# The 16 token-mixing gates of a decoder layer as pairs by a seven-product block scheme

## The chip, the cores and the metric

The kernel runs on one core of one Trainium2 chip. The metric is the device time of one execution in microseconds. The engines that the text names: PE (TensorE, matrix products, with weight loads shown apart as PEld), DVE (VectorE), ACT (ScalarE), POOL (GpSimd), and SP (SyncE), which issues most of the transfers. Each engine works off its own instructions in a fixed order.

## The reference, cut to what matters

One decoder layer for a prompt of 512 tokens with 16 meta tokens and for 8 short samples. The normalised input x (1024 channels) goes through one input projection `w_in`, from which differential attention and a gated delta rule with four heads are computed. Each of the two branches is projected back to 1024 channels, and both are merged by two gates per channel, which come from the same projection:

```python
z = x @ w_in                          # one projection, split into nine parts
...
gate_a, gate_b = sigmoid(z[C_GA:]), sigmoid(z[C_GB:])   # 1024 channels each
mix = gate_a * (attention @ w_branch_a) + gate_b * (delta_rule @ w_branch_b)
```

An output projection, and then a gated feed-forward layer with a short convolution, follow. The kernel takes the sigmoid by a tanh of half the argument. All is float32. So the gates are one matrix product: 2048 output channels by 1024 input channels by 578 tokens.

## The kernel before, in words

Tokens are columns, channels are partitions. There are 578 columns, kept in two halves: columns 0 to 256, and 256 to 578 (322 of them). A float32 value is held as the sum of two numbers of the shorter matmul format, hi and lo. `split` makes them: ACT casts the value to hi, and DVE subtracts hi from it to give lo (`whi` and `wlo` for weights, `xhi` and `xlo` for the input x). A product of 128 input channels with 128 output channels is then three matmuls: hi by hi, hi by lo and lo by hi. For 1024 input channels that makes 24 matmuls for each half of the tokens.

`gate(i)` computes 128 of the 2048 gate channels. It fetches the weights with two transfers of 256 KB (`wraw`), splits them, multiplies both halves into two accumulator banks of the kind "d" (`ps_d`; two exist in this stage), and ACT takes the tanh into a tile `gt`. There are 16 such columns, two for each of 8 output blocks m.

The order of the program is set in two steps. Two streams are merged while the program is written (`merge`): `main` with the attention prompt and then the four heads of the delta rule, and `rest` with the attention of the samples, the 16 gates, and `branch_a`, the branch projection of the attention. `merge` takes the next step from the stream that is furthest behind by estimated work, and passes over a stream that announced a delay. After that a list scheduler places each engine's instructions. The gates are mostly the work that fills PE while a head's chain of small dependent steps waits for other engines.

A head is two streams of its own: `gdn_project(h)` makes its queries, keys and values, and `gdn_chain(h)` does the rest. In the chain come Gram products of keys (`ps_g`), masks by decay on DVE (`dbig_low`, `dbig_up`, `lm`), a triangular substitution on DVE (the loop of L970 to L972 on `row` and `xc`, 15 rounds, each needing the one before), products with its result `xy` on PE, a recurrence over chunks (`gv`, `gS`, `grhs`, `st`), normalisation of the output `on`, transposes of it, and multiplication by the head's own gate z, which `gdn_gate` computes from x with 48 matmuls. The product `ob` is then split (`bhi`, `blo`). For each head, `gdn_gate` is called near the chain's end, ahead of the transposes of `on` in program order.

The input x as hi and lo lies in `self.x` and stays there until the gates are done. While head h's chain runs, `gdn_project(h + 1)` uses the buffers `pre`, `cy`, `q`, `kt` and `vt`; during the last head's chain they are free. `branch_a` puts the splits of the attention result `oa` into `pre`, `cy`, `q` and `qb`.

The feed-forward stage (`ffn_in`) already multiplies in blocks of two by two with seven products in place of eight; the sums of weight blocks it needs (`sw`, L1805) are made on POOL and DVE, and split afterwards (`hw`, `lw`).

Of the kernel before, what the change touches and what calls it, by code (L numbers as in the profile page):

```python
# [9 lines left out]
F32 = mybir.dt.float32  # L10
F32R = mybir.dt.float32r
I32 = mybir.dt.int32
AF = mybir.ActivationFunctionType
ALU = mybir.AluOpType
# [11 lines left out]
H = 4  # L26
# [8 lines left out]
NQ = SEQ + NS + 2  # L35
# [4 lines left out]
HALF_Q = ((0, 256), (256, 578))  # L40
# [99 lines left out]
WRAW, WLO = 3, 4  # L140
LOADS_AHEAD = 5
NC = 290
PLAIN = 3
TAILS = 4
FINE = 8
MAIN_1 = 600.0
# [4 lines left out]
class Body:  # L151
# [39 lines left out]
    def run(self):  # L191
        nc, ctx = self.nc, self.ctx
        self.cpool = self.pool(ctx, "cpool")
        self.wpool = self.pool(ctx, "wpool")
        self.small = self.pool(ctx, "small")
        self.dram = self.pool(ctx, "dram", space=bass.MemoryType.DRAM)
        self.consts = self.t(self.cpool, [128, _CONSTANTS.shape[1]], "consts")
        self.ident = self.consts[:, 0:128]
        nc.scalar.dma_start(self.ident, self.a["constants"][:, 0:128])
        self.mhalf = self.t(self.cpool, [128, 32], "mhalf")  # L200
        nc.vector.memset(self.mhalf, -0.5)
        self.x2d = self.t(self.dram, [NQ, D], "x2d")

        self.psum = self.pool(ctx, "psum", space=PSUM)
        self.banks, self.turn = "d", 0
        with ExitStack() as sm:
            with ExitStack() as s1:
                self.opool = self.pool(s1, "opool")
                self.oa = self.t(self.opool, [128, H, NQ], "oa")
                self.ob = self.t(self.opool, [128, H, NQ], "ob")  # L210
                with ExitStack() as s2:
                    self.keep = self.pool(s2, "keep")
                    self.x = self.parts(self.pool(s2, "xpool"), "x", 8, HALF_T)
                    with ExitStack() as s:
                        first = self.embed(self.pool(s, "embed", 2, side="right"))
                    self.gproj = self.pool(s2, "gproj")
                    da = ExitStack()
                    dpool = self.pool(da, "da")
                    self.psum_m = self.pool(da, "psum_m", space=PSUM)
                    self.da_queries(dpool, first)  # L220
                    with ExitStack() as s:
                        tmp = self.pool(s, "gs", side="right")
                        self.gdn_scalars(tmp)
                        self.gdn_consts(tmp)
                    self.news = self.chain = self.spare = False

                    def main():
                        head = {}
                        yield from self.da_main(dpool, self.gdn_project(0, head))
                        da.close()  # L230
                        self.chain = True
                        self.psum_g = self.pool(ctx, "psum_g", space=PSUM)
                        with ExitStack() as s:
                            self.gpool = self.pool(s, "gpool")
                            yield from self.gdn(head)
                        yield from self.mix_parts(self.pool(s2, "mix"))

                    def rest():
                        with ExitStack() as s:
                            yield from self.sample_attention(self.pool(s, "sa", side="right"))  # L240
                        self.gates, self.gtpool = {}, self.pool(sm, "gates", side="right")
                        for i in range(16):
                            yield from self.gate(i)
                        while not self.spare:
                            yield None
                        yield from self.branch_a()

                    self.drain(self.merge((main(), lambda: MAIN_2 if self.chain else MAIN_1), (rest(), REST_W)))
                    self.banks = "ggsttdd"
                    swo = ExitStack()  # L250
                    wo0 = self.wout_tiles(self.pool(swo, "wo0", side="right"), 0)
                    self.mix(wo0)
            sf = ctx.enter_context(ExitStack())
            fx = self.pool(sf, "fx")
            self.f = {
                key: tuple(self.t(fx, [128, 4, NC], f"f{p}{key}", F32R) for p in ("hi", "lo")) for key in ("11", "12", "21", "22")
            }
            for key in ("12", "22"):
                for e in self.f[key]:
                    nc.scalar.copy(e[:, :, 32:34], self.c("zero").unsqueeze(2).to_broadcast([128, 4, 2]))  # L260
            with ExitStack() as s:
                firsts = self.out_proj(self.pool(s, "wout"), wo0, swo, sm)
            self.ffn_in(firsts, sf, self.pool(sm, "gx", side="right"))
            sf.close()
            with ExitStack() as s1:
                self.ffn_out(self.pool(s1, "gh"), self.pool(s1, "fo"), self.pool(s1, "w3"))
# [399 lines left out]
    def gdn(self, head):  # L666
        pool = self.gpool
        self.zk = self.t(pool, [128, NB * 136], "zk")
        self.nc.gpsimd.memset(self.zk, 0.0)
        heads = [head] + [{} for _ in range(H - 1)]  # L670
        for h in range(H):
            streams = [(self.gdn_chain(h, heads[h]), 29.4)]
            if h + 1 < H:
                streams.append((self.gdn_project(h + 1, heads[h + 1]), 18.0))
            yield from self.merge(*streams)

    def gdn_project(self, h, st):
# [22 lines left out]
    def gdn_gate(self, h, z2):  # L700
        nc = self.nc
        wt = self.weight(self.a["w_in"][0], C_Z + 128 * h)
        for half in HALF_Q:
            out = []
            yield from self.dense_steps(wt, self.x, half, out)
            for p, c in out:
                zh = z2[:, c[0] : c[1]]
                nc.scalar.activation(zh, p, AF.Tanh, scale=0.5)
                nc.vector.scalar_tensor_tensor(out=zh, in0=zh, scalar=1.0, in1=p, op0=ALU.add, op1=ALU.mult)
            yield 0.0  # L710

    def gdn_chain(self, h, st):
        nc, pool, a, o = self.nc, self.gpool, self.a, self.o
        q, kt, vt = st["q"], st["kt"], st["vt"]
        C4 = [128, 4, 128]

        def cols(ap, h=h):
# [7 lines left out]
            out=gu, in0=self.c("upper").unsqueeze(1).to_broadcast(C4), in1=cols(self.g), op=ALU.mult  # L725
# [9 lines left out]
        for big, sign in (("big_low", -1.0), ("big_up", 1.0)):  # L735
            m = self.t(pool, [NTL, NTL], "dt" + big)
            nc.vector.scalar_tensor_tensor(
                out=m, in0=rt[:NTL, :NTL], scalar=self.gc[:NTL, 4, h : h + 1], in1=self.c(big + "_t", NTL),
# [9 lines left out]
        for big, sign in (("big_low", -1.0), ("big_up", 1.0)):  # L748
            m = self.t(pool, C4, "d" + big)
# [3 lines left out]
        last = self.t(pool, [128, 12], "elast")  # L753
# [32 lines left out]
        for e in range(2):  # L786
# [7 lines left out]
            out=kn[:, 0:4], in0=kn[:, 0:4], in1=kc[:, 0:4].unsqueeze(2).to_broadcast(C4), op=ALU.mult  # L794
        )
        yield DELAY[4]
        p = self.ps("t")
# [3 lines left out]
        p = self.ps4("t")  # L801
# [24 lines left out]
        y, at = res["yt"], res["att"]  # L826
        p = self.ps("g")
        for b in range(NB):
# [5 lines left out]
            out=rhs[:64], in0=p[:64, :128], scalar=self.neg_eg[:64, 4, h : h + 1], in1=vn[:64, 4],  # L834
# [6 lines left out]
        p = self.ps("g")  # L841
        self.mm(p[:NTL, :128], y, rhs[:NTL], start=True, stop=True)
        v = self.t(pool, [128, 128], "gv", bufs=2)
        nc.scalar.copy(v[:NTL], p[:NTL, :128])
        yield DELAY[7]
        p = self.ps("g")
# [3 lines left out]
        p = self.ps("g")  # L850
# [7 lines left out]
        for half in range(2):  # L858
# [3 lines left out]
                out=vm[:64],  # L862
                in0=v[:64].unsqueeze(1).to_broadcast([64, 4, 128]),
                in1=self.c("blocks_s", 64)[:, b4].unsqueeze(2).to_broadcast([64, 4, 128]),
                op=ALU.mult,
# [11 lines left out]
        for i in range(4):  # L877
            sl = slice(128 * i, 128 * i + 128)
            p = self.ps("g")
# [3 lines left out]
                out=rhs, in0=p[:, :128], scalar=self.neg_eg[:, i, h : h + 1], in1=vn[:, i], op0=ALU.mult, op1=ALU.add  # L883
# [30 lines left out]
            out=on[:, 0:4], in0=on[:, 0:4], in1=f[:, 0:4].unsqueeze(2).to_broadcast(C4), op=ALU.mult  # L914
        )
        nc.vector.tensor_scalar(on[:NTL, 4], on[:NTL, 4], f[:NTL, 4:5], None, op0=ALU.mult)
        z2 = self.t(pool, [128, NQ], "z2")
        yield from self.gdn_gate(h, z2)
        p = self.ps4("t")
        for i in range(4):  # L920
            self.transpose(p[:, i], on[:, i])
# [563 lines left out]

    GATES = ((C_GB, "w_branch_b"), (C_GA, "w_branch_a"))

    def gate(self, i):
        m, j = divmod(i, 2)
        th = self.t(self.gtpool, [128, NQ], "gt", bufs=18)  # L1490
        wt = self.weight(self.a["w_in"][0], self.GATES[j][0] + 128 * m)
        for half in HALF_Q:
            out = []
            yield from self.dense_steps(wt, self.x, half, out, 4)
            for p, c in out:
                self.nc.scalar.activation(th[:, c[0] : c[1]], p, AF.Tanh, scale=0.5)
            yield 0.0
        self.gates[i] = th

    def branch(self, m, j, x, half):  # L1500

# [707 lines left out]
```

## Time and profile before

| | |
|---|---|
| time, median of three runs | 1155.24 us (1153.86 to 1158.56) |
| the profiled execution | 1153.75 us, its span 1152.0 us |
| granted clock, mean | 0.996 |
| PE busy | 1115.3 us of the span |
| gates (tanh of the first to that of the last) | 493.6 to 620.4 us |
| feed-forward, the stretches of it read below | 800 to 1000 us |

A row of a group names line, engine, operation, output and inputs by the program's names, shape and count; then follow the busy time in total and the mean duration in nanoseconds, and then idle time of the engine before these instructions with what ended it. A row of a timeline begins with the start time and the duration in microseconds; a bracket at its end gives the idle time before it. A row of the stretches gives, for a window of the span, its length and each engine's busy time, the granted TensorE clock, and the transfers' share and rate.

### The profile page before, as it was taken

The numbers are of one execution on the slowest core, as the hardware profiler recorded it, in microseconds if no ns is written. First come the engines' busy times: TensorE is split into PE (matmuls) and PEld (weight loads), VectorE is DVE, ScalarE is ACT, GpSimd is POOL, SyncE is SP. The second block draws the span as 40 slices with busy tenths as digits, with TensorE's granted clock in tenths as the row PEclk, the third lists the DMA queues.
The fourth block names the chain that finished last, engine by engine and source line by source line (L and its number), as shares of the span: only waits on it lengthen the run. The fifth ranks groups of instructions, "written<-read, shape, count | busy, mean of one in ns | idle before, by whom it ended". The sixth has DMA issues, their size and how long they took to land.

```text
span 1152.0 us, 23616 instructions
## 1 busy us (share of the span) xinstructions
PE 1115.3 (97%) x8683; PEld 1004.1 (87%) x8683; DVE 717.3 (62%) x1875; ACT 539.0 (47%) x1308; POOL 220.5 (19%) x342
## 2 busy tenths in 40 slices
PE   6999999999999999999999999999999999999997
PEld 5887887787787787789999977899999999999996
DVE  5456666695486377474343765499889889832323
ACT  5334445464464365352332344365565656732321
POOL 2022221020120010010000003333455444200000
PEclk9999999999999999999999999999999999999999
DMA  7366335737756956823232364323333332432322
GB/s 208 81 223 188 102 104 195 255 110 251 237 159 216 290 173 209 263 74 80 55 90 69 110 187 153 95 70 102 102 87 100 93 94 73 144 97 74 102 75 83
DMA packets 184347, 157.56 MB, mean 137 GB/s; under 512 B 12570, under 2 KB 146273, under 8 KB 184231
## 3 DMA queue, kind: packets, MB, share of 16 engines
q1 hardware_dynamic: 179713, 147.53, 42.0%
q0 software_dynamic: 3264, 5.16, 1.5%
q10 hardware_dynamic: 1254, 3.35, 1.0%
q8 instruction: 69, 1.13, 0.4%
q14 instruction: 47, 0.39, 0.1%
HBM read 146.12 MB, written 9.88 MB: 135 GB/s over the span
## 4 chain that ended last, share of the span: by engine, by line
PE 73%; issue 13%; DVE 6%; ACT 3%; POOL 3%; DMA 1%; SPq 0%; DVEq 0%; POOLq 0%; ACTq 0%
PE ps_d L272 26%; PE ps_t L272 18%; PE ps_g L272 15%; PE ps_s L272 7%; PE ps_t L420 7%; ACT KT L1399 1%; PE ps_m L272 1%; DVE cy L650 1%; DMA lk<-in_da_lambda_k 1%; POOL grr L384 1%; POOL gf L384 0%; DVE wlo L315 0%; DMA page<-in_cache_v 0%; POOL hss L384 0%; DVE row L970 0%
## 5 line engine op out<-in xcount | busy, mean ns | idle before, releaser
L272 PE MATMUL ps_d<-xhi,whi 128*128 128x256 f32 (+2 forms) x704 | 217.8, 310 | 0.2 <-DVE qm L1128 0.2
L315 DVE TENSOR_TENSOR wlo<-wraw,whi 128x512 fp32r<-128x512 f32 x196 | 137.9, 720 | 122.4 <-ACT whi L314 121.6
L272 PE MATMUL ps_d<-xhi,wlo 128*128 128x256 f32 (+2 forms) x704 | 213.3, 303 | 0.7 <-DVE wlo L315 0.7
L272 PE MATMUL ps_d<-xlo,whi 128*128 128x256 f32 (+2 forms) x704 | 212.8, 303 | 0.3 <-DVE xlo L315 0.2
L314 ACT CAST whi<-wraw 128x512 fp32r<-128x512 f32 (+1 forms) x198 | 117.3, 612 | 179.1 <-PE ps_d L272 93.8
L272 PEld LDWEIGHTS ps_d<-xhi,whi 128*128 128x128 f32 x704 | 133.6, 190 | 5.8 <-issue 4.2
L272 PEld LDWEIGHTS ps_d<-xlo,whi 128*128 128x128 f32 x704 | 133.9, 190 | 3.3 <-issue 2.4
L272 PEld LDWEIGHTS ps_d<-xhi,wlo 128*128 128x128 f32 x704 | 133.6, 190 | 2.5 <-issue 1.0
L1399 ACT COPY KT<-ps_t 128x512 f32<-128x512 f32 x106 | 57.2, 603 | 31.3 <-PE ps_t L420 30.8
L420 PE MATMUL ps_t<-consts,page 128*128 128x128 f32 x512 | 67.8, 279 | 0.3
L272 PE MATMUL ps_t<-fhit,hw 128*128 128x290 f32 x228 | 68.0, 298 | 0.0
L272 PE MATMUL ps_t<-flot,hw 128*128 128x290 f32 x228 | 67.7, 297 | 0.0
L272 PE MATMUL ps_t<-fhit,lw 128*128 128x290 f32 x228 | 67.6, 297 | 0.0
L420 PEld LDWEIGHTS ps_t<-consts,page 128*128 128x128 f32 x512 | 55.6, 140 | 13.8 <-issue 6.7
L314 ACT CAST hw<-sw 128x512 fp32r<-128x512 f32 x76 | 47.2, 622 | 41.4 <-PE ps_g L272 19.9
L315 DVE TENSOR_TENSOR lw<-sw,hw 128x512 fp32r<-128x512 f32 x76 | 60.1, 790 | 6.7 <-ACT hw L314 6.6
L272 PEld LDWEIGHTS ps_t<-flot,hw 128*128 128x128 f32 x228 | 43.2, 190 | 0.0
L272 PEld LDWEIGHTS ps_t<-fhit,lw 128*128 128x128 f32 x228 | 43.1, 189 | 0.0
L272 PEld LDWEIGHTS ps_t<-fhit,hw 128*128 128x128 f32 x228 | 43.0, 189 | 0.0
L1887 DVE SCALAR_TENSOR_TENSOR fy<-fpre,fw,fy 128x592 f32<-128x592 f32 x44 | 36.5, 830 | 2.5 <-ACT fy L1885 1.8
L272 PE MATMUL ps_s<-page,pT 128*32 128x256 f32 x512 | 35.3, 385 | 1.8 <-DMA page<-in_cache_v 1.6
L272 PE MATMUL ps_s<-KT,qb 128*32 128x256 f32 x512 | 35.7, 385 | 0.6
(688 smaller groups left out, 2990.1 us busy)
## 6 DMA issues: line engine op xcount, KB each, us to landing
page<-in_cache_k SPq DMA_DIRECT2D x128, 256.0 KB, 4.2
page<-in_cache_v SPq DMA_DIRECT2D x128, 256.0 KB, 4.4
wraw<-in_w_in SPq DMA_DIRECT2D x88, 256.0 KB, 3.0
wraw<-in_w_ffn_in SPq DMA_DIRECT2D x50, 256.0 KB, 3.0
wraw<-in_w_down SPq DMA_DIRECT2D x40, 256.0 KB, 3.2
raw<-in_w_ffn_in SPq DMA_DIRECT2D x38, 256.0 KB, 2.9
wraw<-in_w_out SPq DMA_DIRECT2D x16, 256.0 KB, 2.9
x<-in_x_prompt SPq DMA_DIRECT2D x4, 512.0 KB, 8.7
```

Of the source, the lines that this page charges most:

```text
L272: return self.nc.tensor.matmul(out, lhsT, rhs, **kw).ins
L314: self.nc.scalar.copy(hi, raw)
L315: (eng or self.nc.vector).tensor_tensor(out=lo, in0=raw, in1=hi.bitcast(F32), op=ALU.subtract)
L384: nc.gpsimd.tensor_tensor(out=dst, in0=dst, in1=self.mhalf[:rows, :n], op=ALU.pow)
L420: self.nc.tensor.transpose(out, in_, self.ident[:k, :k])
L650: nc.vector.scalar_tensor_tensor(out=y, in0=pre[:, j : j + n], scalar=self.cw[:, ch, 24 + j : 25 + j], in1=y, op0=ALU.mult, op1=ALU.add)
L1399: copy(kt[:, :, 128 * j : 128 * j + 128], tp)
L1887: nc.vector.scalar_tensor_tensor(out=y, in0=pre[:, j : j + 592], scalar=fw[:, m, 16 + j : 17 + j], in1=y, op0=ALU.mult, op1=ALU.add)
```

## The change

The gates are computed in pairs of columns (2n, 2n+1) by a block scheme of seven products. The weights of a pair are four blocks: lower and upper half of the input channels for each of the two columns. The tokens are two blocks, X1 (columns 256 to 578, of which the first 256 take part in the scheme) and X2 (columns 0 to 256), again with lower and upper channels.

In round 1, `begin(n)` multiplies the lower half of column 2n with X1 into a bank and ACT copies this to the tile of column 2n+1; `end(n)` adds the upper half onto the same bank, and ACT takes the tanh, which finishes columns 256 to 578 of column 2n. Meanwhile POOL computes sums and differences of the token blocks (`sums`, `more`), first in rooms borrowed from `pre`, `cy`, `q`, `qb` and two gate tiles; they are split into `t3`, the `vt` buffer, and x's own blocks, which they overwrite (the scheduler orders this behind the last use).

In round 2, POOL makes four sums of weight blocks for each pair (`loads`), each is split as before (`divided`), and five products follow: two into bank A with 322 columns, one with 256, and two into bank C (`ps_s`) with 256. After each of them DVE adds the bank, as far as it has come, to what stands in the tiles (L1645, L1648, L1651, L1654, L1658), and ACT takes the remaining tanhs. The weights of round 2 are fetched a second time, with four transfers of 256 KB for each pair.

Since x is overwritten, head 3's own gate has to be computed before: `last_gate` runs as a stream beside the beginning of head 3's chain, and `rest` waits for it (`self.free`) before any gate is begun. The unchanged matmul helper, L272 before, has line 275 after; `split` moves from L314 and L315 to L317 and L318.

```diff
@@ constants
+AHEAD = 1
@@ run
-                        for i in range(16):
-                            yield from self.gate(i)
+                        while not self.free:
+                            yield None
+                        with ExitStack() as s:
+                            yield from self.all_gates(self.pool(s, "t3", side="right"))
@@ gdn
                 streams.append((self.gdn_project(h + 1, heads[h + 1]), 18.0))
+            else:
+                streams.append((self.last_gate(heads[h]), 18.0))
@@
+    def last_gate(self, st):
+        st["z2"] = self.t(self.gpool, [128, NQ], "z2")
+        yield from self.gdn_gate(H - 1, st["z2"])
+        self.free = True
@@ gdn_chain
-        z2 = self.t(pool, [128, NQ], "z2")
-        yield from self.gdn_gate(h, z2)
+        z2 = st.get("z2")
+        if z2 is None:
+            z2 = self.t(pool, [128, NQ], "z2")
+            yield from self.gdn_gate(h, z2)
@@
-    def gate(self, i):
...
-            yield from self.dense_steps(wt, self.x, half, out, 4)
-            for p, c in out:
-                self.nc.scalar.activation(th[:, c[0] : c[1]], p, AF.Tanh, scale=0.5)
+    def all_gates(self, pool):
...
+        def product(ps, wt, x, n, first, last, k0=0):
...
+            for k in range(4):
+                self.mm(ps[:, :n], hi[k], xhi[k0 + k][:, 0:n], start=first and k == 0, stop=False, **kw)
+                self.mm(ps[:, :n], hi[k], xlo[k0 + k][:, 0:n], start=False, stop=False, **kw)
+                self.mm(ps[:, :n], lo[k], xhi[k0 + k][:, 0:n], start=False, stop=last and k == 3, **kw)
...
+        def sums(e):
...
+            op(r12, raw(h2, ks, c), raw(l2, ks, c), ALU.add)
+            op(r11, raw(h1, ks, c), raw(l1, ks, c), ALU.add)
+            op(r11, r12, r11)
+            yield
+            op(r22, raw(h2, us, c), raw(l2, us, c), ALU.add)
+            op(r12, r22, r12)
+            op(r22, r22, r11)
+            yield
+            self.split(t3[e], t3[2 + e], r12)
+            self.split(h2[:, ks, c], l2[:, ks, c], r11)
+            op(r21, raw(h1, us, c), raw(l1, us, c), ALU.add)
+            op(r21, r21, r22)
+            yield
+
+        def later(e, j):
...
+            self.split(h1[:, ks, c], l1[:, ks, c], r)
...
+        def begin(n):
+            wt = self.weight(w, column(2 * n))
+            ps = self.ps("d")
+            product(ps, (wt[0][:4], wt[1][:4]), X1, N1, True, True)
+            nc.scalar.copy(th[2 * n + 1][:, 256:NQ], ps[:, :N1])
+            p1s[n] = ps, wt
+
+        def end(n):
+            ps, wt = p1s.pop(n)
+            product(ps, (wt[0][4:], wt[1][4:]), X1, N1, False, True, 4)
+            nc.scalar.activation(th[2 * n][:, 256:NQ], ps[:, :N1], AF.Tanh, scale=0.5)
+
+        def loads(n):
...
+            op(s1, a21, a22, ALU.add)
+            op(a21, a11, a21)
+            op(a11, s1, a11)
+            op(a12, a12, a11)
+            return {"s1": s1, "s3": a21, "s2": a11, "s4": a12, "22": a22}
+
+        begin(0)
+        yield 0.0
+        for n in range(1, 8):
+            begin(n)
+            yield 0.0
+            next(work, None)
+            next(work, None)
+            if n == 5:
+                ready.append(loads(0))
+            if n == 7:
+                for e in range(2):
+                    later(e, 0)
+            end(n - 1)
+            yield 0.0
...
+        end(7)
+        yield 0.0
+        for e in range(2):
+            later(e, 1)
+        self.split(h1[:, upper, c], l1[:, upper, c], more)
...
+        for n in range(8):
+            A, C = self.ps("d"), self.ps("s")
...
+            product(A, next(wts), X1, N1, True, True)
+            v.tensor_tensor(out=b1, in0=A[:, :N2], in1=p1, op=ALU.add)
+            yield 0.0
+            product(C, next(wts), X2, N2, True, True)
+            v.tensor_tensor(out=b2, in0=C[:, :N2], in1=p1, op=ALU.add)
+            yield 0.0
+            product(A, next(wts), X3, N2, False, True)
+            v.tensor_tensor(out=b2, in0=A[:, :N2], in1=b2, op=ALU.add)
+            yield 0.0
+            product(C, next(wts), X2, N2, False, True, 4)
+            v.tensor_tensor(out=b1, in0=C[:, :N2], in1=b1, op=ALU.add)
+            nc.scalar.activation(b1, b1, AF.Tanh, scale=0.5)
+            yield 0.0
+            product(A, next(wts), X1, N1, False, True, 4)
+            v.tensor_tensor(out=t2[:, 256:NQ], in0=A[:, :N1], in1=t2[:, 256:NQ], op=ALU.add)
+            nc.scalar.activation(t2, t2, AF.Tanh, scale=0.5)
+            yield 0.0
```

Three places of the two programs' orders are shown in the prediction. Names there are those of the program with running numbers; two names that differ only in the number are two buffers or two uses of one.

80 lines of the change are left out of this document (73 added, 7 removed).

## The prediction, made before the changed kernel was run

> **What bounds the kernel now.** I read the page first, then a table of stretches, TensorE's waits, and last single stretches as timelines. Busy times of the page:
>
> ```profile
> PE 1115.3 (97%) x8683; PEld 1004.1 (87%) x8683; DVE 717.3 (62%) x1875; ACT 539.0 (47%) x1308; POOL 220.5 (19%) x342
> ```
>
> TensorE (PE) works for 1115.3 of 1152.0 us, so work taken from it counts unless a new wait replaces it. The table of stretches covers the gates, 493.6 to 620.4 us by the last row of the next fence, and the feed-forward stage, which already multiplies by the seven-product scheme:
>
> ```profile
> core 0: us, PE busy (x) PEld busy (x) DVE busy (x) ACT busy (x) POOL busy (x), PEclk, DMA share, GB/s
> 490.00:500.00 10.00, 8.73 (x64) 7.69 (x63) 8.33 (x26) 6.62 (x20) 1.80 (x2) 1.00 0.26 63
> 500.00:550.00 50.00, 49.77 (x382) 49.07 (x381) 29.25 (x102) 17.66 (x51) 2.90 (x2) 1.00 0.29 74
> 550.00:600.00 50.00, 50.00 (x380) 47.70 (x379) 17.62 (x39) 16.83 (x49) 2.70 (x3) 1.00 0.30 76
> 800.00:900.00 100.00, 100.00 (x745) 99.96 (x744) 89.34 (x160) 59.50 (x109) 49.17 (x68) 1.00 0.32 92
> 900.00:1000.00 100.00, 100.00 (x743) 99.92 (x742) 89.29 (x161) 63.43 (x117) 44.02 (x63) 1.00 0.32 95
> ...
> L1496 ACT ACTIVATE gt<-ps_d x32: 361/413/442, 493.6 to 620.4; 128x256 f32<-128x256 f32 x16, 128x322 f32<-128x322 f32 x16
> ```
>
> PE is full in the gates, at granted clock 1.00, with VectorE (DVE) at 29.25 and 17.62 of 50 us and GpSimd (POOL) nearly idle. The feed-forward rows show the scheme running with PE at 100.00 while DVE is at 89 of 100. The one long wait near the gates is this, the idle time before head 3's transposes:
>
> ```profile
> 492.87 0.73 PE L420 MATMUL ps_t<-consts,on 128*128 128x128 f32 x5 [1.27 <-DVE on L913]
> ```
>
> **What it removes.** A pair of gate columns cost 48 matmuls of 256 columns and 48 of 322; now it costs 48 of 322 (24 in each round) and 36 of 256. That is 12 fewer for each of eight pairs, 96 in all. Their price is the start-to-start spacing in a full stretch:
>
> ```profile
> 600.77 0.28 PE L272 MATMUL ps_d<-xlo,whi 128*128 128x256 f32 x1
> ...
> 602.90 0.28 PE L272 MATMUL ps_d<-xlo,whi 128*128 128x256 f32 x1
> ...
> 603.49 0.31 PE L272 MATMUL ps_d<-xhi,whi 128*128 128x322 f32 x1
> ...
> 605.57 0.31 PE L272 MATMUL ps_d<-xhi,wlo 128*128 128x322 f32 x1
> ```
>
> From 600.77 to 602.90 are 18 steps: 0.118 us each. From 603.49 to 605.57 are 14: 0.149 us each. So 96 x 0.118 = **11.4 us** leaves PE. The Trainium skill ("TensorE: Matmul & The Clock Gate", section "Back-to-back issue gap") gives columns / 2.4 GHz plus about 2.5 ns, by which a matmul of 256 columns would be 109 ns and the gain 10.5 us; the trace's spacing is longer, and I keep it.
>
> **What it adds, and where.** The durations, by shape:
>
> ```profile
> L315 DVE TENSOR_TENSOR wlo<-wraw,whi 128x512 fp32r<-128x512 f32 x188 | 135.1, 732 | 121.5 <-ACT whi L314 120.7
> L315 DVE TENSOR_TENSOR lw<-sw,hw 128x512 fp32r<-128x512 f32 x76 | 60.1, 790 | 6.7 <-ACT hw L314 6.6
> L1841 DVE TENSOR_TENSOR fpre<-ps_d,p 128x258 f32<-128x258 f32 x19 | 8.1, 426 | 5.2 <-PE ps_d L272 5.0
> L1805 POOL TENSOR_TENSOR sw<-raw,raw 128x512 f32<-128x512 f32 x19 | 24.9, 1312 | 25.7 <-DVE lw L315 24.5 <-DMA raw<-in_w_ffn_in 1.2
> L314 ACT CAST whi<-wraw 128x512 fp32r<-128x512 f32 x190 | 114.7, 621 | 177.9 <-PE ps_d L272 93.8 <-PE ps_t L272 18.0 <-PE ps_g L272 15.6
> L1834 ACT COPY u<-ps_t 128x290 f32<-128x290 f32 x19 | 7.5, 397 | 0.0
> ```
>
> *Round 1, first five pairs.* Begin and end of a pair use two accumulator banks, each held until its tanh is through. The matmuls of head 3's chain and of attention stand between and fill; in the rows above (500 to 550 us) PE loses 0.23 us of 50 with two banks. I take +0.8 us (0 to 2).
>
> *Round 1, last three pairs.* Behind head 3's first Gram products PE has nothing but gates. In PE's order, an old column there:
>
> ```order
> L272 MATMUL ps_d_7379<-xhi_8_87,whi_7334 128x322
> L272 MATMUL ps_d_7379<-xlo_9_88,whi_7334 128x322
> L272 MATMUL ps_d_7379<-xhi_8_87,wlo_7338 128x322
> L272 MATMUL ps_d_7496<-xhi_6_85,whi_7489 128x256
> L272 MATMUL ps_d_7496<-xlo_7_86,whi_7489 128x256
> L272 MATMUL ps_d_7496<-xhi_6_85,wlo_7490 128x256
> ```
>
> And in the changed kernel, where ps_d_7651 is pair 6's bank and ps_d_7604 pair 5's:
>
> ```order
> L275 MATMUL ps_d_7651<-xhi_8_87,whi_7644 128x322
> L275 MATMUL ps_d_7651<-xlo_9_88,whi_7644 128x322
> L275 MATMUL ps_d_7651<-xhi_8_87,wlo_7645 128x322
> L275 MATMUL ps_d_7604<-xhi_8_87,wlo_7601 128x322
> L275 MATMUL ps_d_7651<-xhi_8_87,whi_7644 128x322
> L275 MATMUL ps_d_7651<-xlo_9_88,whi_7644 128x322
> L275 MATMUL ps_d_7651<-xhi_8_87,wlo_7648 128x322
> ```
>
> The old rows go from bank to bank and wait for nothing new. Now the second half of a pair accumulates onto a bank that ACT must first copy out, with a single matmul between: tail 0.31, copy about 0.43 (0.397 for 290 columns), two hand-overs of about 0.04, less two steps of 0.149, is 0.52 us; three such pairs, the last partly covered, make 1.3 us.
>
> The same stretch fills DVE. It holds the triangular substitution (L970 to L972), 15 rounds one behind another:
>
> ```profile
> 510.15 0.23 DVE L941 TENSOR_TENSOR dtbig_low<-ps_g,dtbig_low 80x80 f32<-80x80 f32 x1
> ...
> 521.38 0.68 DVE L315 TENSOR_TENSOR wlo<-wraw,whi 128x512 fp32r<-128x512 f32 x1
> 521.98 0.20 DVE L971 TENSOR_TENSOR row<-row,lc 128x45 f32<-128x45 f32 x1
> ...
> 527.86 0.68 DVE L982 TENSOR_TENSOR xy<-xc,consts 128x512 f32<-128x512 f32 x1
> ...
> 540.45 1.01 PE L272 MATMUL ps_t<-consts,xy 128*128 128x32 f32 x8
> ```
>
> It ends at 528.5 and PE asks for it at 540.45: 12 us of slack. From 510.15 it takes 18.4 us, in which five foreign operations stand; a split there holds DVE for 0.60 us (521.38 to 521.98), so the substitution alone needs about 18.4 - 3.0 = 15.4 us. DVE's order, before and after, near its end:
>
> ```order
> L970 STREAM_SHUFFLE row_7424<-xc_7413 128x5x9
> L315 TENSOR_TENSOR wlo_7618<-wraw_7613,whi_7617 128x512
> L971 TENSOR_TENSOR row_7424<-row_7424,lc_7411 128x5x9
> L972 TENSOR_TENSOR xc_7413<-xc_7413,row_7424 128x5x9
> L315 TENSOR_TENSOR wlo_7621<-wraw_7615,whi_7617 128x512
> L970 STREAM_SHUFFLE row_7424<-xc_7413 128x5x10
> ```
>
> ```order
> L982 STREAM_SHUFFLE row_7505<-xc_7494 128x5x14
> L318 TENSOR_TENSOR xlo_9_88<-qb_7249,xhi_8_87 128x2x256
> L983 TENSOR_TENSOR row_7505<-row_7505,lc_7492 128x5x14
> L318 TENSOR_TENSOR wlo_7771<-pre_7245,whi_7770 128x512
> L984 TENSOR_TENSOR xc_7494<-xc_7494,row_7505 128x5x14
> L318 TENSOR_TENSOR xlo_9_88<-gt_7250,xhi_8_87 128x2x256
> L982 STREAM_SHUFFLE row_7505<-xc_7494 128x5x15
> L318 TENSOR_TENSOR xlo_9_88<-more_7272,xhi_8_87 128x4x66
> L983 TENSOR_TENSOR row_7505<-row_7505,lc_7492 128x5x15
> L1645 TENSOR_TENSOR gt_7256<-ps_d_7739,gt_7257 128x256
> L984 TENSOR_TENSOR xc_7494<-xc_7494,row_7505 128x5x15
> ```
>
> Some 16 foreign operations now stand in it: splits of round 1's weights, of the token sums, of round 2's first weights, and round 2's first add. At 0.60 us that is 9.6 us, in all 25.0 us of DVE against 25.1 us of PE work (169 steps of 0.149). DVE is then as late as PE; queued behind it are the weight splits that PE waits for. Going through both orders row by row, each operation at its duration, I find about 2.7 us of weight waits in pairs 4 to 7 and 0.35 for the first add. Slower splits come on top:
>
> ```profile
> 899.94 0.69 DVE L315 TENSOR_TENSOR lw<-sw,hw 128x512 fp32r<-128x512 f32 x1
> 901.49 1.05 DVE L315 TENSOR_TENSOR lw<-sw,hw 128x512 fp32r<-128x512 f32 x1
> ...
> 900.71 1.28 POOL L1805 TENSOR_TENSOR sw<-raw,raw 128x512 f32<-128x512 f32 x1 [1.32 <-DVE lw L315]
> ```
>
> The same split takes 0.69 alone and 1.05 us beside a POOL sum. The sums add some 50 POOL operations to the stage; for the few in this stretch I add 1.0 us. Together round 1's last pairs cost 1.3 + 2.7 + 0.35 + 1.0 = **+5.4 us** (1.3, the copies alone, to 10, all 16 contended).
>
> *Round 2.* A pair is 24 x 0.149 + 36 x 0.118 = 7.8 us of PE. DVE owes it five splits (5 x 0.79 = 3.95), four adds of 0.42 and one of about 0.49, 6.1 us, and some 1.3 us of head 3's chain: 95% of PE's time, a little over the feed-forward stage's 89. Ahead of a product on a bank in use an add must be done: tail 0.31, hand-over 0.04, add 0.42, of the 12 x 0.118 = 1.42 us of the product between. So 0.65 us is free, and a split of 0.69 to 1.05 us that stands just before costs 0.04 to 0.40 us. I take one of 0.28 a pair, **+2.2 us** (0, as in the feed-forward stage, to 16, 40 splits at 0.40). POOL's four sums of 1.31 us fit in 7.8, ACT's five casts of 0.62 and two tanhs (0.41 for up to 322 columns) too.
>
> *Last pair.* Head 3's four output splits now stand ahead of its first add:
>
> ```order
> L318 TENSOR_TENSOR wlo_8648<-qb_7249,whi_8631 128x512
> L318 TENSOR_TENSOR blo_1631_8579<-ob_78,bhi_1630_8578 128x578
> L318 TENSOR_TENSOR blo_1633_8583<-ob_78,bhi_1632_8582 128x578
> L318 TENSOR_TENSOR blo_1635_8587<-ob_78,bhi_1634_8586 128x578
> L318 TENSOR_TENSOR blo_1637_8591<-ob_78,bhi_1636_8590 128x578
> L1645 TENSOR_TENSOR gt_7270<-ps_d_8629,gt_7271 128x256
> ```
>
> Before, no accumulator waited behind them. Four at the split's 0.73 are about 3 us, against 0.65 free and what has run by then: **+1.6 us** (0 to 3).
>
> *Moved gate.* Head 3's own gate costs the same at either end; at the chain's beginning six more matmuls of 322 columns stand ahead of the transposes at 492.87, 6 x 0.149 = 0.9 of the 1.27 us: **-0.9 us** (0 to -1.3). At its end the chain is not missed: gates and branch work lie behind it. The splits of oa that go to the end of round 2 are due only after the gates: 0. Of the 48 weight transfers (32 before) none should be late: the DMA share is 0.29.
>
> **Sum.** -11.4 + 0.8 + 5.4 + 2.2 + 1.6 - 0.9 = -2.3 us. The profiled execution took 1153.75 us (span 1152.0 and 1.75 around it), so 1151.4; the median of the runs, 1155.24, lies 1.5 higher, so **1153 us**.
>
> **Rivals.**
> (A) The waits are hidden. For it: the feed-forward rows, PE at 100.00 beside DVE at 89. Against: that stage has no substitution on DVE, and no copy between two halves on one bank. Then -11.4 - 0.9 + 2 (copies and some rest): 1145 us. Chance 0.30.
> (B) DVE becomes the bound, slower. Place: round 2's adds and the substitution. If 40 adds meet contended splits, 40 x 0.40 = 16 in place of 2.2: +11.5, 1167 us. It decides once the stage's waits pass the 11.4 us saved plus the bound below. For it: 95% by count; against: the feed-forward rows. Chance 0.20.
> (C) POOL and DVE exclude each other: then a round-2 pair needs 6.1 + 1.3 + 5.2 = 12.6 us of the two, 4.8 over PE's 7.8, and eight pairs lose 38 us: about 1190 us. DVE 89.34 and POOL 49.17 in one stretch of 100 us exclude it nearly. The Trainium skill ("GPSIMD Engine Reference", section "1. Specifications") says that POOL's memory interfaces are shared with DVE, with contention for DVE operations with two inputs in SBUF, which every split is; the trace has that as 1.05 for 0.69 us, not as exclusion. Chance 0.02.
>
> **Chances and range.** The forecast, most of the saving spent on DVE's and the copies' waits (1149.5 to 1161), has 0.46; 0.02 is left for what I don't see. Half a per cent, 5.8 us, is about what a measurement of this kernel tells from no change. Faster by more: A and a little, 0.31; slower by more: B, C and a little, 0.23; within: 0.46. The range goes from 1144 (A with nearly nothing lost) to 1167 (B's price).
>
> **What would show it.** Right: PE's waits of about 0.5 us on ACT's copies in round 1, waits on wlo there, DVE near full from the Gram products to the first pair of round 2, 256-column spacing still 0.118. Wrong: PE at 100% from round 1's end (A), or waits on the adds in every pair of round 2 and wlo means near 1.0 us (B), or late weight transfers, which I cost at nothing.

## The result, and the profile after

The changed kernel takes 1173.17 us (median of four runs, 1170.99 to 1174.92) against 1155.38 us for the kernel before (1153.86 to 1158.56): a ratio of 1.0152, 95% interval 1.0134 to 1.0170. It is 17.8 us slower where 2 us less was forecast.

The profiled execution has a span of 1168.7 us, 16.7 more than before. The page's busy times:

```profile
PE 1113.6 (95%) x8587; PEld 997.6 (85%) x8587; DVE 779.7 (67%) x1948; ACT 561.4 (48%) x1341; POOL 293.9 (25%) x393
```

There are 96 fewer matmuls (8587 for 8683), so the work did go. But PE's busy time fell by only 1.7 us, and the time in which PE does nothing rose from 36.7 to 55.1 us. PE's waits from 380 to 760 us, grouped (total, times, longest):

```profile
PE ps_d L275 <- DVE wlo L318: 5.2, 3, 2.9
PE ps_s L275 <- DVE row L983: 3.5, 1, 3.5
PE ps_t L423 <- DVE on L923: 2.9, 2, 2.0
PE ps_d L275 <- DVE gt L1645: 2.1, 2, 1.1
PE ps_s L275 <- DVE gt L1648: 1.6, 1, 1.6
PE ps_d L275 <- DVE xc L984: 1.3, 1, 1.3
PE ps_t L423 <- DVE kn L802: 1.3, 1, 1.3
```

Nearly all of them end on DVE. The stretches explain most of the missing fall in busy time (PE, PEld, DVE, ACT, POOL busy, granted clock, transfers):

```profile
440.00:444.00 4.00, 1.36 (x16) 0.69 (x16) 3.94 (x13) 0.00 (x0) 1.25 (x2) 0.82 0.64 214
444.00:448.00 4.00, 3.99 (x39) 2.85 (x32) 2.90 (x19) 2.19 (x4) 0.79 (x2) 0.76 0.41 132
500.00:504.00 4.00, 4.00 (x16) 2.86 (x15) 2.93 (x9) 2.46 (x6) 0.13 (x1) 0.57 0.20 48
520.00:524.00 4.00, 4.00 (x22) 3.98 (x21) 3.99 (x5) 1.42 (x4) 3.92 (x3) 0.63 0.59 131
524.00:528.00 4.00, 3.90 (x28) 3.60 (x27) 3.97 (x8) 0.99 (x2) 1.66 (x2) 0.94 0.09 12
540.00:544.00 4.00, 3.29 (x14) 2.89 (x15) 3.56 (x19) 1.06 (x3) 0.00 (x0) 0.69 0.52 131
544.00:548.00 4.00, 4.00 (x25) 3.81 (x23) 2.63 (x10) 2.73 (x6) 0.00 (x0) 0.89 0.45 115
...
580.00:600.00 20.00, 20.00 (x162) 19.13 (x162) 15.56 (x29) 10.62 (x27) 9.00 (x7) 1.00 0.35 83
600.00:620.00 20.00, 19.32 (x140) 17.61 (x138) 15.78 (x30) 9.82 (x24) 13.06 (x9) 1.00 0.42 115
```

Before, the clock was 1.00 through this stage, in the first two of these windows too (kernel before):

```profile
440.00:444.00 4.00, 3.94 (x41) 2.94 (x42) 3.57 (x23) 2.39 (x5) 1.02 (x2) 1.00 0.96 345
444.00:448.00 4.00, 3.95 (x43) 3.02 (x41) 3.40 (x23) 2.96 (x7) 0.00 (x0) 1.00 0.93 312
```

Now it is lowered in four places, each right after one of the longer waits (those ending at 442.64, 498.85, 519.67 and 540.46 us). The missing clock in the first seven rows, (0.18 + 0.24 + 0.43 + 0.37 + 0.06 + 0.31 + 0.11) x 4 us, is 6.8 us: four stretches that cost 1.7 us each. In round 2's body (last two rows) PE is nearly as full as before.

What holds DVE shows when DVE's and POOL's timelines of the changed kernel are laid side by side. In head 3's substitution (start, duration):

```profile
533.65 1.27 DVE L984 TENSOR_TENSOR xc<-xc,row 128x15 f32<-128x15 f32 x1
...
535.17 1.12 DVE L983 TENSOR_TENSOR row<-row,lc 128x20 f32<-128x20 f32 x1
...
536.54 0.20 DVE L982 STREAM_SHUFFLE row<-xc 128x25 f32<-128x25 f32 x1
536.78 0.93 DVE L983 TENSOR_TENSOR row<-row,lc 128x25 f32<-128x25 f32 x1
...
538.21 0.90 DVE L983 TENSOR_TENSOR row<-row,lc 128x30 f32<-128x30 f32 x1
...
533.60 1.29 POOL L1529 TENSOR_TENSOR q<-pre,wraw 128x512 f32<-128x512 f32 x1 [7.87 <-issue]
534.97 1.29 POOL L1529 TENSOR_TENSOR pre<-pre,pre 128x512 f32<-128x512 f32 x1
536.33 1.34 POOL L1529 TENSOR_TENSOR pre<-q,pre 128x512 f32<-128x512 f32 x1
537.75 1.31 POOL L1529 TENSOR_TENSOR cy<-cy,pre 128x512 f32<-128x512 f32 x1
```

The same DVE operation in the kernel before:

```profile
517.62 0.17 DVE L972 TENSOR_TENSOR xc<-xc,row 128x15 f32<-128x15 f32 x1
```

A DVE operation of 0.17 us takes 1.27 us, and ends at 534.92, when POOL's sum ends at 534.89. The next ends at 536.29 (POOL 536.26), the next at 537.71 (537.67), then 539.11 (539.06). These operations aren't slowed beside POOL; DVE stands still with them until POOL is through. The shuffle at 536.54 isn't held: it ends while POOL's sum runs. Which other operations this hits shows a little earlier:

```profile
523.26 1.20 DVE L847 COPY grhs<-vn 16x128 f32<-16x128 f32 x1
524.49 0.24 DVE L953 TENSOR_TENSOR dtbig_low<-ps_g,dtbig_low 80x80 f32<-80x80 f32 x1
524.80 1.04 DVE L969 TENSOR_TENSOR lbt<-dtbig_low,consts 80x80 f32<-80x80 f32 x1
...
522.54 1.84 POOL L1529 TENSOR_TENSOR gt<-gt,q 128x512 f32<-128x512 f32 x1
524.46 1.28 POOL L1529 TENSOR_TENSOR gt<-gt,gt 128x512 f32<-128x512 f32 x1
```

A copy from SBUF (the memory that holds the tiles, apart from the accumulator banks) and an operation on two operands in SBUF wait. The one that reads an accumulator bank (524.49) runs through in 0.24 us, while a POOL sum runs (524.46 to 525.74). And POOL waits in its turn where DVE was first: 1.84 us for 1.28.

### The profile page after: what moved, and what is told of

Its sections match the earlier page's. It is cut to its first block, busy times and chain, and to the rows that moved or that the text cites. A ratio compares the mean times of both kernels' runs of the same rounds, so it can differ in the third digit from the quotient of the medians.

```text
span 1168.7 us, 23657 instructions
## 1 busy us (share of the span) xinstructions
PE 1113.6 (95%) x8587; PEld 997.6 (85%) x8587; DVE 779.7 (67%) x1948; ACT 561.4 (48%) x1341; POOL 293.9 (25%) x393
## 4 chain that ended last, share of the span: by engine, by line
PE 72%; issue 12%; DVE 8%; POOL 3%; ACT 3%; DMA 1%; DVEq 0%; POOLq 0%; ACTq 0%; SPq 0%
PE ps_d L275 23%; PE ps_t L275 18%; PE ps_g L275 15%; PE ps_s L275 8%; PE ps_t L423 7%; DVE wlo L318 1%; PE ps_m L275 1%; ACT KT L1411 1%; POOL grr L387 1%; DVE cy L653 1%; DVE row L983 1%; POOL gf L387 0%; DVE xc L984 0%; DMA page<-in_cache_v 0%; DVE xlo L318 0%
## 5 line engine op out<-in xcount | busy, mean ns | idle before, releaser
L318 DVE TENSOR_TENSOR wlo<-wraw,whi 128x512 fp32r<-128x512 f32 (+1 forms) x188 | 136.5, 742 | 90.6 <-ACT whi L317 89.7
L317 ACT CAST whi<-wraw 128x512 fp32r<-128x512 f32 (+1 forms) x190 | 112.7, 614 | 156.9 <-PE ps_d L275 76.3
L275 PE MATMUL ps_d<-xhi,wlo 128*128 128x256 f32 (+2 forms) x576 | 178.2, 311 | 6.4 <-DVE wlo L318 6.2
L275 PE MATMUL ps_d<-xhi,whi 128*128 128x256 f32 (+2 forms) x576 | 181.8, 316 | 1.0 <-ACT gt L1575 0.9
L275 PE MATMUL ps_d<-xlo,whi 128*128 128x256 f32 (+2 forms) x576 | 177.6, 309 | 0.3 <-DVE xlo L318 0.2
L275 PEld LDWEIGHTS ps_d<-xhi,wlo 128*128 128x128 f32 x576 | 110.0, 191 | 9.8 <-DVE wlo L318 8.2
L275 PEld LDWEIGHTS ps_d<-xhi,whi 128*128 128x128 f32 x576 | 110.2, 192 | 6.8 <-issue 3.8
L275 PEld LDWEIGHTS ps_d<-xlo,whi 128*128 128x128 f32 x576 | 110.1, 191 | 4.1 <-issue 3.1
L423 PEld LDWEIGHTS ps_t<-consts,page 128*128 128x128 f32 x512 | 56.2, 142 | 14.1 <-issue 7.1
L317 ACT CAST hw<-sw 128x512 fp32r<-128x512 f32 x76 | 47.3, 624 | 41.6 <-PE ps_g L275 20.1
L318 DVE TENSOR_TENSOR lw<-sw,hw 128x512 fp32r<-128x512 f32 x76 | 59.5, 783 | 6.8 <-ACT hw L317 6.7
```

Of the source, the lines that this page charges most:

```text
L275: return self.nc.tensor.matmul(out, lhsT, rhs, **kw).ins
L317: self.nc.scalar.copy(hi, raw)
L318: (eng or self.nc.vector).tensor_tensor(out=lo, in0=raw, in1=hi.bitcast(F32), op=ALU.subtract)
L423: self.nc.tensor.transpose(out, in_, self.ident[:k, :k])
```

## The experiments

Theory L: POOL and DVE shut each other out of SBUF, and the 51 POOL sums make DVE late where a chain or PE needs it. Rival W: DVE has too much work (splits, adds, bank turns), and POOL doesn't matter. Costs below are against the kernel before, from the measured ratio of the two kernels times 1154.5 us, with the 95% interval; they can differ by a microsecond from the difference of the medians.

**The sums moved from POOL to DVE.** First the token sums:

```diff
         def sums(e):
+            op = lambda out, a, b, o=ALU.subtract: v.tensor_tensor(out=out, in0=a, in1=b, op=o)
...
-            op(more, raw(h1, upper, c), raw(h1, lower, c))
+            op(more, raw(h1, upper, c), raw(h1, lower, c), eng=v)
...
```

> The changed kernel with the 19 sums of token blocks on DVE in place of POOL; the sums of weight blocks stay on POOL. Theory L (a POOL sum holds off DVE's operations on SBUF until it ends): the waits at 431 and 442 us (1.2 and 3.5 us) and at 519 us (1.95 us) go, and two of the four stretches of halved clock with them (1.7 us each), DVE's own 11 us of sums fall mostly where it has room: 1162 to 1167 us. Rival W (DVE simply has too much work, POOL does not matter): DVE gets 11 us more, 1173 to 1182 us.

Measured 1168.66 us, +14.1 us (10.7 to 17.4): 4.5 us below the changed kernel, a little less than L expected, with intervals that just overlap; W expected slower. The waits at 431, 442 and 519 us are gone, but a row of small ones came in from 490 to 503 us, and there the clock lacks 6.8 us (rows in the last section). With 1.7 us more at 536 to 544 that is 8.5 us, where L had expected two of the changed kernel's four stretches to go. Then pair 0's weight sums too:

```diff
-            op(s1, a21, a22, ALU.add)
+            eng = v if n == 0 else g
+            op(s1, a21, a22, ALU.add, eng)
...
```

> As the kernel before it, and the four weight sums of pair 0 (533 to 539 us, inside head 3's substitution) on DVE too. Theory L: 2.4 us of DVE in place of some 4 us held off; the 2.9 us wait at 540 us shrinks to 1 to 2 and its halved clock goes: 2 to 4 us less than the kernel before it. Rival W: 0 to 3 us more than the kernel before it.

Measured 1165.29 us, +11.2 us (7.7 to 14.8), 3.4 below the one before it. That is the size L has, but the intervals overlap widely, and the trace has another reason for it beside L's. The wait for a weight split (2.92 us at 540 in the changed kernel, 3.20 at 536 in the one before this) is gone, with its 1.7 us of clock; but the missing clock around 500 us, far from these sums, fell too, from 6.8 to 1.7 us. And a new wait of 3.1 us ends at 552.40, on an add (L1653) that itself takes 0.41 us, but stands in DVE's queue behind this, beside POOL's sums for pairs 1 and 2 (DVE timeline of this run):

```profile
548.94 1.78 DVE L318 TENSOR_TENSOR wlo<-wraw,whi 128x512 fp32r<-128x512 f32 x1
550.64 1.27 DVE L984 TENSOR_TENSOR xc<-xc,row 128x60 f32<-128x60 f32 x1
551.84 0.41 DVE L1653 TENSOR_TENSOR gt<-ps_d,gt 128x256 f32<-128x256 f32 x1
```

Then all sums on DVE:

```diff
-            eng = v if n == 0 else g
+            eng = v if True else g
```

> All 51 sums on DVE, none on POOL. Theory L: no POOL operation holds DVE off any more, but a pair of round 2 now costs DVE 5 splits and 4 sums of 0.6, adds of 2.2 and 1.3 of chain, 8.9 us for PE's 7.8, so DVE becomes the bound there: 1163 to 1172 us, with PE waiting evenly for wlo over round 2. Rival W: as many waits as with the sums on POOL and 30 us more of DVE: over 1185 us.

Measured 1166.43 us, +11.8 us (7.7 to 15.7). With some 19 us more work on DVE (28 sums) it is no slower, within the intervals, than the step before, which is against W. DVE's busy time didn't grow either (776.1 us, 777.2 in the step before): the time that the sums now take on DVE is about what DVE had stood still for. But L's place was wrong: PE doesn't wait evenly over round 2. It has one long wait (DVE, ACT and PE timelines of this run):

```profile
545.88 0.69 DVE L1529 TENSOR_TENSOR qb<-qb 128x512 f32<-128x512 f32 x1 [1.45 <-DMA qb<-in_w_in]
...
547.34 0.62 ACT L317 CAST whi<-qb 128x512 fp32r<-128x512 f32 x1 [2.93 <-DVE qb L1529]
...
548.01 0.63 PE L275 MATMUL ps_d<-xhi,whi 128*128 128x322 f32 x1 [4.14 <-ACT whi L317]
```

A sum on DVE waits for its weights' transfer, and everything queued behind it waits as well.

**The sums alone, in the kernel before.** The 16 token sums of 512 columns are added to the kernel before, in the same rooms, results unused:

```diff
+                        work = self.extra(nc.gpsimd)
                         for i in range(16):
                             yield from self.gate(i)
+                            if i:
+                                next(work, None)
...
```

> The kernel before, with 16 sums of token blocks on POOL added into borrowed rooms, results unused, nothing else changed. Theory L: DVE operations beside them stretch to the end of the POOL operation, PE waits about 4 us near 430 to 442 us and 1 to 3 us near 515 us, with one or two stretches of halved clock: +4 to +10 us, 1159 to 1165 us. Rival W: POOL was nearly idle there, nothing waits for these results: within 1.5 us of before.

Measured 1164.71 us, +9.5 us (7.0 to 11.8). Nothing waits for these results, and yet PE waits 1.2, 2.3 and 1.2 us from 432 to 456 us, and here:

```profile
519.29 0.94 PE L275 MATMUL ps_g<-q,kk 128*128 128x128 f32 x6 [3.94 <-DVE dtbig_up L945]
```

Right behind that wait the clock is 0.57 from 520 to 524 us, 1.7 us missing. These four waits and the clock make 10.4 us, about what was measured, so the lock and the clock leave little for another cause.

The same on DVE:

```diff
-                        work = self.extra(nc.gpsimd)
+                        work = self.extra(nc.vector)
```

> The same 16 sums added to the kernel before, but on DVE (16 x 0.6 us). Theory L: DVE has room, 0 to +3 us, less than with the sums on POOL. Rival W: +3 to +10 us, more than with the sums on POOL.

Measured 1159.98 us, +5.0 us (3.3 to 6.6): half of the cost on POOL, as L has it, but more than the 0 to 3 expected. The Gram wait at 520 us is back to 0.23; a row of small waits stands at 494 to 502 us, beginning with this:

```profile
494.46 0.49 PE L275 MATMUL ps_g<-grhs,xy 128*128 128x128 f32 x2 [0.45 <-DVE grhs L885]
```

The sums stand inside head 2's substitution, so I queued them behind it:

```diff
+            with self.tc.issue_after(self.marks[2]):   # the operation right behind head 2's substitution
+                eng.tensor_tensor(out=out, in0=a, in1=b, op=o)
...
```

> The kernel before plus the 16 sums on DVE (which cost 5 us), now queued on DVE behind the end of head 2's substitution. If the 5 us came from head 2's chain being late, and its recurrence so losing its filling work at 494 to 502 us: within 1.5 us of before, and these waits gone. If DVE's time itself is the cost: +4 to +6 us again.

Measured 1157.21 us, +3.8 us (2.0 to 5.7). The small waits are gone, but the time fell less than that, the interval overlaps the earlier one, and 3.8 lies between the two values expected, so it decides for neither. Some 1.7 us of it is clock, 0.71 and 0.87 from 496 to 504 us, behind the wait of 1.24 us on `on` that the kernel before has too (1.27) without a lowered clock. The rest of the cost of DVE sums stays unexplained.

**POOL operations of one operand.** The 16 sums on POOL become copies:

```diff
-            eng.tensor_tensor(out=out, in0=a, in1=b, op=o)
+            eng.tensor_copy(out, a)
```

> The kernel before plus 16 POOL copies of one operand, of the same size and in the same rooms as the 16 sums of the earlier run (which cost 9.5 us). Theory L1 (any POOL operation on SBUF holds DVE off while it runs): DVE operations stretch to the end of the copy, and the cost goes with the copies' duration: for copies half as long +3 to +6 us. Theory L2 (only POOL operations of two operands do): within 1.5 us of before, no DVE operation stretched.

Measured 1156.86 us, +3.7 us (1.5 to 5.9). POOL and DVE in this run:

```profile
428.62 0.62 POOL L1502 COPY pre<-xhi 128x512 f32<-128x512 f32 x1
...
428.59 1.21 DVE L810 TENSOR_TENSOR kn<-kn,ek 128x512 f32<-128x512 f32 x1
```

In the run with sums the same two took 1.28 and 1.89 us. DVE is held by a copy too, for as long as the copy runs: L1 by the trace (the interval's low end alone just touches L2's 1.5). The copies are half as long (0.62 for 1.28) and cost four tenths.

**Sums left out.** These kernels no longer compute the layer, and only their times are of use. First without the token sums:

```diff
-            op(r12, raw(h2, ks, c), raw(l2, ks, c), ALU.add)
...
-            self.split(t3[e], t3[2 + e], r12)
-            self.split(h2[:, ks, c], l2[:, ks, c], r11)
+            self.split(t3[e], t3[2 + e], raw(h2, ks, c))
+            self.split(h2[:, ks, c], l2[:, ks, c], raw(h1, ks, c))
...
```

> The changed kernel with the sums of token blocks left out; the splits that followed them read blocks of x instead, as many and as large. Weight sums stay on POOL. Theory L: the waits at 431, 442 and 519 us go, and DVE has no sums either; what stays is the substitution beside the first pairs' weight sums: 1158 to 1163 us. Rival W (splits, adds and banks are to blame): 1168 to 1174 us.

Measured 1163.89 us, +9.8 us (6.7 to 13.0), just above what L expected. Without the weight sums, the token sums back:

```diff
-            op(s1, a21, a22, ALU.add)
-            op(a21, a11, a21)
-            op(a11, s1, a11)
-            op(a12, a12, a11)
-            return {"s1": s1, "s3": a21, "s2": a11, "s4": a12, "22": a22}
+            return {"s1": a22, "s3": a21, "s2": a11, "s4": a12, "22": a22}
```

> Weight sums left out, token sums as in the changed kernel on POOL. Theory L: the waits at 431 to 442 and 519 us and two stretches of halved clock stay, those from 533 to 568 us (2.9, 1.3, 1.0 and 1.6 us, one halved stretch) mostly go: 1163 to 1168 us. Rival W: 1170 us or more.

Measured 1160.18 us, +7.2 us (4.0 to 10.3), some 3 less than L expected: the weight sums cost more than I had put on them. With both edits:

> Token sums and weight sums both left out, the splits read the unsummed blocks; every matmul, split, add and transfer stays. Theory L: the scheme without POOL, 11.4 us saved less 3 to 7 us of waits on ACT's copies and on DVE during the substitution: 1147 to 1152 us. Rival W: 1163 us or more.

Measured 1152.26 us, ratio 0.9997 (0.9981 to 1.0012), so -0.3 us (-2.2 to +1.4). Its page and waits:

```profile
PE 1107.5 (96%) x8587; PEld 993.0 (87%) x8587; DVE 750.5 (65%) x1948; ACT 559.1 (49%) x1341; POOL 218.7 (19%) x342
...
PE ps_d L275 <- DVE gt L1630: 1.5, 2, 1.1
PE ps_t L423 <- DVE kn L802: 1.2, 1, 1.2
PE ps_d L275 <- ACT gt L1564: 0.9, 3, 0.5
PE ps_d L275 <- DVE wlo L318: 0.2, 1, 0.2
```

Every matmul, split, add and transfer is still there; the clock isn't lowered in this stage, and the kernel ties with the one before. DVE's count of operations is that of the changed kernel (1948), its busy time 29.2 us less: with the same operations, that is time DVE stood still for POOL. The parts add up: weight sums 9.8 + 0.3 = 10.1, token sums 7.2 + 0.3 = 7.5, together 17.6, and with the -0.3 of this kernel 17.3 us, where the changed kernel's ratio gives 17.5 (15.5 to 19.6). In the profiled executions the changed kernel's span is 20.8 us longer than this one's: 14.7 us of it is PE doing nothing, 6.1 us PE's longer busy time, which the 6.8 us of missing clock cover. W falls.

Leaving a sum out also takes out the wait for its result. For the token sums the run with unused results has no such wait and cost 9.5 us, so the lock alone is enough for their 7.5. For the weight sums no run separates the two. And the sums aren't free on DVE: all 51 there cost 11.8 + 0.3 = 12.1 us against 17.6 on POOL.

**The moved gate alone**, in the kernel before:

```diff
+                        while not self.free:
+                            yield None
                         for i in range(16):
                             yield from self.gate(i)
...
+            else:
+                streams.append((self.last_gate(heads[h]), 18.0))
...
```

> The kernel before with only head 3's own gate moved to its chain's beginning and the gates waiting for it. The prediction's term: -0.9 us, within 1.5 us of before. Rival R (the move takes filling work from the end of head 2's chain and the beginning of head 3's): +2 to +4 us, with waits on kn and on near 494 to 512 us.

Measured 1155.93 us, +2.4 us (0.8 to 4.0). The gain of 0.9 us is excluded, and the waits are where R has them, though the interval reaches below R's 2. The wait on `on` didn't shrink (1.45 for 1.27), and a new one came:

```profile
510.54 0.63 PE L422 MATMUL ps_t<-consts,kn 128*128 128x128 f32 x4 [0.91 <-DVE kn L802]
```

**The best of these together**: the second kernel above, with the token sums queued behind head 2's substitution:

```diff
-            op = lambda out, a, b, o=ALU.subtract: v.tensor_tensor(out=out, in0=a, in1=b, op=o)
+            def op(out, a, b, o=ALU.subtract):
+                with self.tc.issue_after(self.marks[2]):
+                    v.tensor_tensor(out=out, in0=a, in1=b, op=o)
...
```

> The changed kernel with the token sums and pair 0's weight sums on DVE (1165 us so far), the token sums queued behind head 2's substitution. If the waits at 492 to 503 us go: 1157 to 1161 us, still slower than before, since pair 1's and 2's weight sums on POOL still stand beside head 3's substitution. If not: 1164 to 1167 us.

Measured 1164.51 us, +10.5 us (7.7 to 13.3): no gain over 1165.29. The small waits of 0.35 to 0.45 us before 497 us are gone, but PE now waits 1.7 and 2.2 us for weight splits at 517 and 527 us and 1.9 us for an add at 553 us, and the clock lacks 6.8 us in all. Since even the scheme without any sums only ties, no placing of the sums that I know of would make it faster than the kernel before.

## Why the prediction was wrong, step by step

The step that failed is the price of POOL's sums: "Slower splits come on top" with +1.0 us. The runs show 17.6 us in its place, waits and lowered clock together. The row behind it was right in front of me: a split of 0.69 us that took 1.05 beside a POOL sum. I read it as a split slowed by half. But it started at 901.49 while the sum ran from 900.71 to 901.99, and it ended at 902.54, so it stood for 0.50 us and then ran for 0.55. What looks like a slowdown of 0.36 us is a wait whose length is whatever POOL has left, and it falls on an operation of 0.18 us as on one of 0.68.

Rival C had this mechanism and was given 0.02, on the ground that DVE 89.34 and POOL 49.17 of 100 us can't exclude each other. They can: in the feed-forward stage part of DVE's operations read accumulator banks, which the changed kernel's trace shows to be free of it (before, at 900.98, one of 256 columns took its usual 0.42 us beside the sum that starts at 900.71), and DVE's busy time contains its standing. C's price (38 us over round 2) was as wrong as its chance. Round 2's adds read banks, and a pair lasted 11.3 us and not 7.8 (first adds from 554.1 to 633.0 us, seven pairs apart), as PE did other work between, so there was room; PE lost most of its time around the substitutions of heads 2 and 3. The Trainium skill ("SBUF — State Buffer", section "SBUF: two separate sides") says it plainly: the shared port pair is an exclusive lock held for the whole instruction, against DVE operations in a two-port mode or with two inputs in SBUF. The ends at 534.92 and 534.89 agree.

The other terms, by the run without sums:

- The saving was 96 matmuls, as counted. In that run's profile PE's busy time fell by 7.8 us, not 11.4 (in the changed kernel by 1.7, and 6.8 of clock make 8.5); where the other 3.6 went I have not traced.
- Copies between two halves on one bank: 0.9 us in three waits, 1.3 forecast. First add: 0.37 us, 0.35 forecast. Last pair: 1.09 us, 1.6 forecast.
- Weight waits beside the substitution: 0.2 us, 2.7 forecast. Round 2's adds: no wait, 2.2 forecast. Both were too dear.
- The moved gate: +2.4 us, -0.9 forecast. The matmuls put ahead of the transposes were missing elsewhere.
- The lowered clock, 6.8 us in the profiled execution, is in no term. I costed waits at their length; each of the four longest brought 1.7 us on top.

Without sums the forecast would have been about 3 us less than before and the run says -2.2 to +1.4; so the scheme's own sum came near, but partly by luck: weight waits and adds were 4.7 us too dear, the moved gate and the removed work 6.9 us too favourable. Rival A (all waits hidden, 1145 us) fails even there. Rival B's time (1167) was nearest, but its place was not: adds in round 2 made PE wait in two of eight pairs only (0.97 and 1.60 us in the second, 1.09 in the last), and a weight split took 742 ns in the mean, where B had near 1.0 us.

## What to carry to other kernels

Before giving work to an idle POOL, look at what DVE does at that time: here each POOL operation stopped DVE's copies and two-operand work in SBUF for its full length, so a chain of small DVE operations pays up to 1.3 us for each sum of 512 columns, where the same sum on DVE holds it for 0.6. POOL freed DVE of next to nothing: DVE's busy time, standing included, is 779.7 us with the 51 sums on POOL and 776.1 with all of them on DVE. When a row shows an operation longer beside another engine, compare its end with the other's end: a short one that ends with the other, or a long one that ends its own length after it, points to a lock, and the busy share of the waiting engine then counts waiting. And waits of PE in a full stretch should be costed with the clock that they may take down, 1.7 us a time here, though not behind every wait.

## What the runs showed of the hardware

- POOL and DVE exclude each other on SBUF for whole operations, POOL copies of one operand included (DVE 1.21 us beside a copy of 0.62, 1.89 beside a sum of 1.28), but not for every DVE operation. In the changed kernel an operation on two operands in SBUF (1.27 us for 0.17), a copy (1.20 at 523.26 for 0.22 at 442.61) and one with a scalar (`kn`, 1.30 at 521.24 for 0.28 at 426.76) were held. One with an operand in an accumulator bank (0.24 us), a shuffle (0.20) and a reduction (1.01 us at 436.37, beside a sum from 435.79 to 437.09; 1.04 in the kernel before) were not.
- In the changed kernel four waits of 1.95 to 3.5 us were each followed by a lowered clock worth 1.7 us; waits of 1.3 and 1.6 us, at 554 and 568 us, were not. The other runs show that the length of a wait doesn't decide this. One of 1.24 us (DVE sums queued later; clock 0.71 and 0.87 from 496 to 504) and one of 1.77 us (no token sums; 0.57 from 496 to 500) were followed by it. One of 2.01 us (no weight sums; 1.00 from 500 to 508) and one of 3.12 us (pair 0's sums on DVE; 1.00 from 552 to 564) were not. So the stretch at 500 us of the changed kernel, behind a wait on `on` that is 1.78 us long without any sums, need not be the sums' doing. The Trainium skill ("TensorE: Matmul & The Clock Gate", section "What's actually happening") gives a window of 3413 ns and an idle window as the cause of half clock. By an estimate from that figure one window at half clock costs 1.7 us, which agrees with the four stretches; but here waits of 1.95 us and less, shorter than the window, were enough. A row of small waits of about 0.4 us, from 490 to 495 us, did the same in the run with the token sums on DVE, for longer:

```profile
492.00:496.00 4.00, 2.84 (x12) 2.25 (x11) 1.41 (x5) 0.72 (x3) 0.00 (x0) 0.64 0.77 222
496.00:500.00 4.00, 3.12 (x8) 1.33 (x8) 1.94 (x10) 1.72 (x6) 1.80 (x2) 0.50 0.13 36
500.00:504.00 4.00, 3.61 (x15) 2.86 (x15) 3.91 (x10) 2.05 (x5) 0.00 (x0) 0.50 0.03 6
504.00:508.00 4.00, 4.00 (x21) 3.97 (x21) 2.30 (x9) 2.29 (x9) 0.00 (x0) 0.65 0.25 66
```

There the clock lacks (0.36 + 0.50 + 0.50 + 0.35) x 4 = 6.8 us. What brings the clock down, a share of idle time or where a wait falls, was not settled.
